# Last of seven products issued behind the next matrix's first product, with the weight factors placed anew

## The chip, the cores and the metric

The kernel runs on one core of one Trainium2 chip. The metric is the device time of one execution in microseconds (us), as the median of several runs; lower is better.

## The reference

The program is one inference step of a two-layer streaming encoder: feed-forward block, mixer, feed-forward block, and the same again with another mixer, on 640 tokens of width 1024. Four of the six sub-layers are feed-forward blocks, and the change lies in these alone. Each computes

```python
D_MODEL = 1024
D_FF = 2816
def swiglu(x, w_gate, w_up, w_down):
    return (jax.nn.silu(x @ w_gate) * (x @ w_up)) @ w_down
```

wrapped as x = LayerNorm(ALPHA * x + 0.5 * swiglu(x)). All arithmetic has float32 accuracy: a float32 factor is split into a high part and the remainder, and a product takes three matmuls (high by high, low by high, high by low).

## The kernel before, in words

The four blocks run one after the other as ffn0, ffn1, ffn2 and ffn3, with a mixer behind ffn0 and one behind ffn2. The hidden width 2816 is 22 rows f of 128 units. Rows 0 and 1 are done with plain products at the start of a block, and so is the gate of rows 2 and 3. Every other gate or up weight of two rows f and f + 1 is what the texts call a *matrix*: a 2 x 2 block problem (two rows of units, two halves of the 1024 inputs, two halves of the 640 tokens) that is done with seven products in place of eight. A block has 19 matrices, the four blocks have 76, and they are numbered here from 0: ffn0 has 0 to 18, ffn1 19 to 37, ffn2 38 to 56, ffn3 57 to 75. The first of each block is the up matrix of rows 2 and 3, and then gate and up alternate.

`operands` (L338) loads the two raw weight rows r0 and r1 (512 KB each, on SyncE's queue) and makes the seven weight factors: four halves as they come (b11, b21, b12, b22), and four differences that VectorE computes in place in the raw tiles (`total`, L348). A factor is then split (L99): ScalarE casts the high part (L100), VectorE subtracts it from the source (L101). `split2` does two factors at once, a cast and a subtraction of 1024 columns. The split factors lie in places that hold two factors each (`two_units`, pool "w", six places) and in one that holds a single factor (`unit`, pool "w1", one place).

`product` (L361) is 12 matmuls of 128 x 128 by 128 x 320 on TensorE (L365), into one PSUM bank. `matrix` (L369) runs the seven products in the order 1, 5, 6, 2, 7, 3, 4 over three banks: x takes products 1 and 2, w takes 5 and later 3, and z begins as a copy of x behind product 1 (`nc.scalar.copy`, L382, ScalarE) and then takes 6, 7 and 4. `keep` (L378) copies a bank to SBUF on ScalarE, behind product 5 and behind product 6. `take` hands a finished quarter to `gate` (add on VectorE, L407, then SiLU on ScalarE, L409) or `up` (L415 to L419, VectorE, and for a finished row its split, L261). The take behind product 7, L407 or L417, reads z, and product 4 then writes on into z. z alternates between two banks (`sums`); x and w come from pool "a", two banks.

`row_sums` (L444) follows an up matrix in ffn1 to ffn3, where the down projection too uses seven products: VectorE forms sums of the finished rows (L453 to L456), ScalarE and VectorE split them into `hs`. `tick` advances side work that ffn0 and ffn3 carry along. `down` (L535; `down7` in the later blocks) runs after every second pair of rows, between a gate and an up matrix. The first down of each block (rows 0 and 1, `tm_proj`, L216) stands directly ahead of the block's first matrix; its results are added to `yacc` on VectorE (L223).

The tile scheduler fixes each engine's order from the order of the code and its own estimate of the times; the engines then run their lists in order and wait for each other by semaphores.

Of the kernel before, what the change touches and what calls it, by code (L numbers as in the profile page):

```python
# [36 lines left out]
def kernel(ctx: ExitStack, tc: tile.TileContext, I, O, phases=PHASES):  # L37
# [45 lines left out]
    state = {"silu": None, "preload": None, "pst": bank_b}  # L83
# [15 lines left out]
    def split(hi, lo, src):  # L99
        nc.scalar.copy(hi, src)  # L100
        return nc.vector.tensor_tensor(lo, src, hi.bitcast(F32), op=ALU.subtract)  # L101

    def raw_tile():
        return pools["raw"].tile([128, 1024], F32, name="raw")
# [7 lines left out]
    def split2(w, src):  # L112

        return split(w[:, :, 0], w[:, :, 1], src.rearrange("p (j c) -> p j c", j=2))
# [111 lines left out]
    def ffn(i, ph, last, side=None):  # L226
# [4 lines left out]
        with ExitStack() as st:  # L231
# [3 lines left out]
            def tick(where):  # L235

                if ph == "ffn0" and where in range(NT):
                    for _ in range(2 if (fs[0], where) == (14, 4) else 1):
                        with tc.issue_after(state["acc"]):
                            next(steps, None)  # L240
                elif ph == "ffn3" and where in ("gate", "up", 0, 2, 4):
                    with tc.issue_after(state["silu"]):
                        next(steps, None)
# [34 lines left out]
            for h in range(2):  # L278
                o, L = HALVES[h]
# [14 lines left out]
            for r in range(2):  # L294
                with tc.issue_after(state["xc"]) if "xc" in state else ExitStack():
                    w = load_w(I["w_gate"][i, 2 + r])
# [41 lines left out]
            def operands(src0, src1):  # L338
                r0, r1 = raw_tile(), raw_tile()
                nc.sync.dma_start(r0, src0)  # L340
                nc.sync.dma_start(r1, src1)
                b11, b21, b12, b22 = r0[:, :512], r0[:, 512:], r1[:, :512], r1[:, 512:]
                u, v, w = (two_units() for _ in range(3))
                o = unit()

                def total(o, v, w):
                    with tc.issue_after(state["lo"]):
                        V.tensor_tensor(o, v, w, op=ALU.subtract)  # L348

                split2(u, r0)  # L350
                state["lo"] = split(v[:, 1, 0], v[:, 1, 1], b22).ins
                total(b11, b12, b11)
                split(v[:, 0, 0], v[:, 0, 1], b11)
                total(b12, b22, b12)
                total(b22, b22, b11)
                split2(w, r1)
                total(b21, b21, b22)
                split(o[:, 0], o[:, 1], b21)
                return {1: u[:, 0], 2: u[:, 1], 3: v[:, 1], 4: o, 5: v[:, 0], 6: w[:, 1], 7: w[:, 0]}

            def product(ps, A, p, first):  # L361
                n = 0
                for k in range(4):
                    for a, b in ((0, 0), (1, 0), (0, 1)):
                        nc.tensor.matmul(ps, A[p][:, a, k * 128:k * 128 + 128], X[p][b][:, k, :],  # L365
                                         start=(first and n == 0), stop=(n == 11), skip_group_check=True)
                        n += 1

            def matrix(A, take):  # L369

                z = sums[0]
                sums.reverse()
                x, w = (bank("a")[:, :Q] for _ in range(2))
                e = {}

                def keep(n, ps):
                    e[n] = wk.tile([128, Q], F32, name="mx", bufs=2)
                    nc.scalar.copy(e[n], ps)  # L378


                product(x, A, 1, True)
                nc.scalar.copy(z, x)  # L382
                product(w, A, 5, True)
                keep(5, w)
                product(z, A, 6, False)
                keep(2, z)
                product(x, A, 2, False)
                take(0, 0, x, None)
                product(z, A, 7, False)
                take(1, 1, z, e[5])  # L390
                product(w, A, 3, False)
                take(1, 0, w, e[2])
                product(z, A, 4, False)
                take(0, 1, z, None)

            def seven(f):
                return ph in SEVEN and f < NF - 4

            def pair(f, before=None):
                g = first if f == 2 else {}  # L400

                def gate(r, c, ps, e):
                    if r not in g:
                        g[r] = g_row()
                    t = g[r][:, Q * c:Q * c + Q]
                    if e is not None:
                        V.tensor_tensor(t, ps, e, op=ALU.add)  # L407
                        ps = t
                    state["silu"] = nc.scalar.activation(t, ps, AF.Silu).ins  # L409

                def up(r, c, ps, e):
                    c = slice(Q * c, Q * c + Q)
                    t = row(f + r)
                    if e is None:
                        V.tensor_tensor(t[:, c], ps, g[r][:, c], op=ALU.mult)  # L415
                    else:
                        V.tensor_tensor(t[:, c], ps, e, op=ALU.add)  # L417
                        if not c.start:
                            V.tensor_tensor(t, t, g[r], op=ALU.mult)  # L419
                    if r == 0 and c.start:  # L420
                        finish(f, *((256, T - 256) if seven(f) else (0, T)))
                    elif r == 1 and not c.start:
                        finish(f + 1)

                for n, take in (("w_gate", gate), ("w_up", up)):
                    if n == "w_gate" and f == 2:
                        tick("gate")
                        continue
                    if n == "w_up" and before is not None:
                        down(before)  # L430
                    with ExitStack() as q:
                        if f == 2:
                            for k in ("acc0", "xc"):
                                if k in state:
                                    q.enter_context(tc.issue_after(state[k]))
                        A = operands(I[n][i, f], I[n][i, f + 1])
                    if n == "w_up":
                        for r in range(2):
                            ht[f + r] = h_tile()
                    matrix(A, take)  # L440
                    if n == "w_up" and seven(f):
                        row_sums(f)
                    tick("gate" if n == "w_gate" else "up")

            hs = {}

# [110 lines left out]
            for c in range(5):  # L557
                done, fs = fs, list(range(2 + 4 * c, 6 + 4 * c))
                for f in fs[::2]:
                    pair(f, done if f == fs[0] else None)  # L560
            state["turn"] = 0
            down(fs, LN_OF[ph])

# [1448 lines left out]
```

## Time and profile before

| what | value |
|---|---|
| time, median of 3 runs | 2542.54 us (2541.85 to 2545.92) |
| time of the profiled execution | 2543.04 us |
| span in the profile | 2541.3 us |
| PE (TensorE matmul) busy | 2500.3 us, 98% of the span |
| DVE (VectorE) busy | 2015.3 us, 79% |
| ACT (ScalarE) busy | 1272.5 us, 50% |
| POOL (GpSimd) busy | 376.2 us, 15% |
| DMA | 324.80 MB, mean 128 GB/s |

A row of the timeline has the start in us from the span's start, the time that the merged instructions take, engine, line, operation, written tile <- read tiles with their shape, the number of instructions, and in brackets the idle time ahead and what ended it. PEld is TensorE's weight load, which runs beside the matmuls.

### The profile page before, as it was taken

The page shows a single profiled execution, that of the slowest core. Times are in us where ns is not written, and L with a number is a line of the kernel's source. Part 1 is how long each engine was busy: PE and PEld are TensorE (multiplying, and loading weights), DVE is VectorE, ACT ScalarE, POOL GpSimd, SP SyncE. Part 2 cuts the span into 40 slices and gives each one's busy share as a digit, 9 for nine tenths or more (in the row PEclk, how much of TensorE's full clock was granted, in tenths as well). Part 3 has the DMA queues.
Part 4 walks back from the last instruction along what each step waited for, and adds up shares of the span by engine and source line. Part 5 has one row for each costly group of instructions (what it writes and reads, how often), then busy time and mean ns, then how long its engine had stood idle before and what let it go on. Part 6 is the DMA issues. An engine that isn't in the chain of part 4 may idle for free. (4 is left out here: it accounts for less than half of the span.)

```text
span 2541.3 us, 40809 instructions
## 1 busy us (share of the span) xinstructions
PE 2500.3 (98%) x15551; PEld 2289.3 (90%) x15551; DVE 2015.3 (79%) x3505; ACT 1272.5 (50%) x2389; POOL 376.2 (15%) x492
## 2 busy tenths in 40 slices
PE   9999999999999999999999999999999999999998
PEld 9999999878789999999999999988989879999897
DVE  7788777666879888878988887777676689998887
ACT  4443444336744555553455554566565544554542
POOL 0000001210130000013000002211121152111121
PEclk9999999999999999999999999999999999999999
DMA  5332335443222433462144434466564722455563
GB/s 185 108 100 86 107 117 154 144 157 110 85 78 65 118 103 97 111 166 62 59 121 112 116 102 125 122 190 184 162 200 138 232 92 91 156 152 163 153 174 115
DMA packets 179253, 324.80 MB, mean 128 GB/s; under 512 B 21312, under 2 KB 92608, under 8 KB 178544
## 3 DMA queue, kind: packets, MB, share of 16 engines
q1 hardware_dynamic: 165200, 293.83, 36.8%
q0 software_dynamic: 13856, 28.35, 5.7%
q8 instruction: 122, 2.00, 0.3%
q14 instruction: 75, 0.61, 0.1%
HBM read 259.56 MB, written 40.54 MB: 118 GB/s over the span
## 5 line engine op out<-in xcount | busy, mean ns | idle before, releaser
L101 DVE TENSOR_TENSOR w<-raw,w 128x512 fp32r<-128x512 f32 (+2 forms) x721 | 625.0, 889 | 87.5 <-ACT w L100 84.7
L100 ACT CAST w<-raw 128x512 fp32r<-128x512 f32 (+1 forms) x721 | 531.8, 769 | 317.2 <-DVE raw L348 153.5
L365 PE MATMUL bank<-xhi,w 128*128 128x320 f32 x2432 | 540.4, 309 | 2.9 <-DVE s L407 1.9
L146 PE MATMUL bank<-xhi,w 128*128 128x256 f32 (+2 forms) x2272 | 499.9, 312 | 2.5 <-ACT xhi L100 1.5
L365 PE MATMUL bank<-T,w 128*128 128x320 f32 x2736 | 428.7, 309 | 3.0 <-ACT bank L382 1.6
L365 PEld LDWEIGHTS bank<-xhi,w 128*128 128x128 f32 x2432 | 406.6, 188 | 8.8 <-DVE s L407 3.1
L365 PEld LDWEIGHTS bank<-T,w 128*128 128x128 f32 x2736 | 407.0, 188 | 6.3 <-ACT bank L382 4.2
L146 PEld LDWEIGHTS bank<-xhi,w 128*128 128x128 f32 x2272 | 380.0, 189 | 11.9 <-issue 5.1
L365 PE MATMUL bank<-xlo,w 128*128 128x320 f32 x1216 | 375.0, 308 | 0.0
L146 PE MATMUL bank<-xlo,w 128*128 128x256 f32 (+2 forms) x1136 | 352.3, 311 | 1.9 <-DVE xlo L211 1.7
L146 PE MATMUL bank<-w,h 128*128 128x512 f32 x1488 | 346.5, 391 | 0.0
L146 PEld LDWEIGHTS bank<-w,h 128*128 128x128 f32 x1488 | 276.9, 188 | 57.6 <-ACT h L100 1.4
L365 PEld LDWEIGHTS bank<-xlo,w 128*128 128x128 f32 x1216 | 228.0, 187 | 0.0
L146 PEld LDWEIGHTS bank<-xlo,w 128*128 128x128 f32 x1136 | 215.0, 189 | 4.9 <-DVE xlo L211 2.0
L348 DVE TENSOR_TENSOR raw<-raw 128x512 f32<-128x512 f32 x304 | 212.4, 699 | 3.4
L514 POOL DMA_DIRECT2D yacc<-ev x84 | 72.7, 889 | 688.2 <-ACT ev L513 603.0
L501 PE MATMUL bank<-w,h 128*128 128x512 f32 x576 | 134.5, 389 | 0.0
L501 PEld LDWEIGHTS bank<-w,h 128*128 128x128 f32 x576 | 108.1, 188 | 22.5
L378 ACT COPY mx<-bank 128x320 f32<-128x320 f32 x152 | 64.6, 425 | 103.7 <-PE bank L365 103.4
L510 DVE SCALAR_TENSOR_TENSOR yacc<-bank,yacc 128x512 f32<-128x512 f32 x84 | 57.8, 688 | 72.2 <-PE bank L501 72.1
L223 DVE SCALAR_TENSOR_TENSOR yacc<-bank,yacc 128x512 f32<-128x512 f32 x120 | 81.8, 686 | 34.3 <-PE bank L146 33.8
L513 ACT ACTIVATE ev<-bank 128x512 f32<-128x512 f32 x84 | 50.1, 597 | 115.8 <-PE bank L501 113.3
(431 smaller groups left out, 3436.7 us busy)
## 6 DMA issues: line engine op xcount, KB each, us to landing
raw<-in_w_gate_dram SPq DMA_DIRECT2D x88, 512.0 KB, 3.7
raw<-in_w_up_dram SPq DMA_DIRECT2D x88, 512.0 KB, 3.9
raw<-in_w_down_dram SPq DMA_DIRECT2D x88, 512.0 KB, 3.6
raw<-in_m_in_dram SPq DMA_DIRECT2D x52, 512.0 KB, 4.6
yacc<-ev POOLq DMA_DIRECT2D x84, 256.0 KB, 4.5
raw<-in_m_out_dram SPq DMA_DIRECT2D x24, 512.0 KB, 4.3
csb<-cs_d SPq DMA_DIRECT2D x20, 512.0 KB, 5.1
h<-in_ssd_h_dram SPq DMA_DIRECT2D x16, 512.0 KB, 6.1
```

Source lines behind the costliest of these rows:

```text
L100: nc.scalar.copy(hi, src)
L101: return nc.vector.tensor_tensor(lo, src, hi.bitcast(F32), op=ALU.subtract)
L146: state["pe"] = nc.tensor.matmul(ps, a, b, start=(k == 0), stop=(k == n - 1)).ins
L223: state["acc"] = nc.vector.scalar_tensor_tensor(ya, pb, scale, ya, op0=ALU.mult, op1=ALU.add).ins
L348: V.tensor_tensor(o, v, w, op=ALU.subtract)
L365: nc.tensor.matmul(ps, A[p][:, a, k * 128:k * 128 + 128], X[p][b][:, k, :], start=(first and n == 0), stop=(n == 11), skip_group_check=True)
L378: nc.scalar.copy(e[n], ps)
L501: nc.tensor.matmul(ps, a[:, u], b[:, v], start=(first and n == 0), stop=(n == 5), skip_group_check=True)
L510: V.scalar_tensor_tensor(ya, ps, 0.5 / ALPHA, ya, op0=ALU.mult, op1=ALU.add)
L513: nc.scalar.mul(e, ps, 0.5 / ALPHA)
L514: nc.gpsimd.dma_start(yacc[:, t, 512 * j:512 * j + 512], e, accum_op=ALU.add)
```

## The change

Product 4 of a matrix, its take and what follows it (row sums, tick) are put into a function, `last_product`, and held in the list `rest`. The next matrix calls it (`complete`) behind its own product 1 and the copy to z, so that TensorE runs 1 of the next matrix, then 4 of this one, then 5 of the next. Ahead of a `down`, and behind the last matrix, `complete` runs at once, so there product 4 stays where it was.

The factors change places. Product 1's factor (b11) moves into the single place; products 2 and 3 share one double place, products 5 and 4 another (one cast and one subtraction of 1024 columns, from r0 after all its differences), products 7 and 6 the third. The four differences now come all in a row, ahead of the two double splits. The counts of splits, differences, matmuls and loads are the same.

```diff
-                split2(u, r0)
-                state["lo"] = split(v[:, 1, 0], v[:, 1, 1], b22).ins
+                split(o[:, 0], o[:, 1], b11)
+                split(u[:, 0, 0], u[:, 0, 1], b21)
+                state["lo"] = split(u[:, 1, 0], u[:, 1, 1], b22).ins
                 total(b11, b12, b11)
-                split(v[:, 0, 0], v[:, 0, 1], b11)
                 total(b12, b22, b12)
                 total(b22, b22, b11)
+                total(b21, b21, b22)
+                split2(v, r0)
                 split2(w, r1)
-                total(b21, b21, b22)
-                split(o[:, 0], o[:, 1], b21)
-                return {1: u[:, 0], 2: u[:, 1], 3: v[:, 1], 4: o, 5: v[:, 0], 6: w[:, 1], 7: w[:, 0]}
+                return {1: o, 2: u[:, 0], 3: u[:, 1], 4: v[:, 1], 5: v[:, 0], 6: w[:, 1], 7: w[:, 0]}
...
-            def matrix(A, take):
+            rest = []
+
+            def complete():
+                if rest:
+                    rest.pop()()
+
+            def matrix(A, take, after):
...
                 product(x, A, 1, True)
                 nc.scalar.copy(z, x)
+                complete()
                 product(w, A, 5, True)
...
-                product(z, A, 4, False)
-                take(0, 1, z, None)
+
+                def last_product():
+                    product(z, A, 4, False)
+                    take(0, 1, z, None)
+                    after()
+
+                rest.append(last_product)
...
                     if n == "w_up" and before is not None:
+                        complete()
                         down(before)
...
-                    matrix(A, take)
-                    if n == "w_up" and seven(f):
-                        row_sums(f)
-                    tick("gate" if n == "w_gate" else "up")
+
+                    def after(up=n == "w_up"):
+                        if up and seven(f):
+                            row_sums(f)
+                        tick("up" if up else "gate")
+
+                    matrix(A, take, after)
...
+            complete()
             state["turn"] = 0
             down(fs, LN_OF[ph])
```

How the instructions stand on the engines, at three places. The first is TensorE in ffn0, at the end of matrix 0 and the start of matrix 1. bank_394 is matrix 0's z, bank_845 (before) or bank_830 (after) matrix 1's x, T1, T2 and T4 are the token factors of products 5, 6 and 3. Before:

```order
240 L365 MATMUL bank_722<-T4_516,w_702 128x320 x12
241 L365 MATMUL bank_394<-xhi_82,w1_704 128x320 x2
242 L365 MATMUL bank_394<-xlo_83,w1_704 128x320
...
249 L365 MATMUL bank_845<-xhi_82,w_827 128x320 x2
250 L365 MATMUL bank_845<-xlo_83,w_827 128x320
...
257 L365 MATMUL bank_846<-T1_514,w_828 128x320 x12
258 L365 MATMUL bank_395<-T2_515,w_829 128x320 x12
```

And after the change:

```order
240 L365 MATMUL bank_722<-T4_516,w_701 128x320 x12
241 L365 MATMUL bank_830<-xhi_82,w1_815 128x320 x2
242 L365 MATMUL bank_830<-xlo_83,w1_815 128x320
...
249 L365 MATMUL bank_394<-xhi_82,w_702 128x320 x2
250 L365 MATMUL bank_394<-xlo_83,w_702 128x320
...
257 L365 MATMUL bank_831<-T1_514,w_813 128x320 x12
258 L365 MATMUL bank_395<-T2_515,w_814 128x320 x12
```

Matrix 0's product 4 into bank_394 moved from ahead of matrix 1's product 1 to behind it: a whole product stands between product 3 and product 4, and two products stand between matrix 1's product 1 and its product 6, which writes the copied z (bank_395).

The second place is VectorE at the start of ffn0's first matrix. raw_697 and raw_698 are r0 and r1; w_701, w_702 and w_703 are the places u, v and w, w1_704 is the single place; yacc is the first down's result. Before:

```order
79 L101 TENSOR_TENSOR w_701<-raw_697,w_701 128x2x512
80 L223 SCALAR_TENSOR_TENSOR yacc_84<-bank_649,yacc_84 128x512
81 L101 TENSOR_TENSOR w_702<-raw_698,w_702 128x512
...
83 L348 TENSOR_TENSOR raw_697<-raw_698,raw_697 128x512
...
87 L101 TENSOR_TENSOR w_702<-raw_697,w_702 128x512
88 L223 SCALAR_TENSOR_TENSOR yacc_84<-bank_681,yacc_84 128x512
89 L348 TENSOR_TENSOR raw_698<-raw_698,raw_697 128x512
90 L223 SCALAR_TENSOR_TENSOR yacc_84<-bank_689,yacc_84 128x512
91 L348 TENSOR_TENSOR raw_697<-raw_697,raw_698 128x512
92 L101 TENSOR_TENSOR w_703<-raw_698,w_703 128x2x512
```

And after the change:

```order
79 L101 TENSOR_TENSOR w1_704<-raw_697,w1_704 128x512
80 L223 SCALAR_TENSOR_TENSOR yacc_84<-bank_649,yacc_84 128x512
81 L101 TENSOR_TENSOR w_701<-raw_697,w_701 128x512
82 L101 TENSOR_TENSOR w_701<-raw_698,w_701 128x512
83 L223 SCALAR_TENSOR_TENSOR yacc_84<-bank_657,yacc_84 128x512
84 L348 TENSOR_TENSOR raw_697<-raw_698,raw_697 128x512
...
90 L348 TENSOR_TENSOR raw_697<-raw_697,raw_698 128x512
91 L223 SCALAR_TENSOR_TENSOR yacc_84<-bank_689,yacc_84 128x512
92 L101 TENSOR_TENSOR w_702<-raw_697,w_702 128x2x512
93 L101 TENSOR_TENSOR w_703<-raw_698,w_703 128x2x512
```

The split that product 5 reads (w_702 from raw_697) moved from row 87, behind one difference, to row 92, behind all four and behind the last accumulation into yacc.

The third place is ScalarE in ffn1, where the row sums of an up matrix (h, ev, hs) meet the gate matrix that follows it; bank_7729 is that gate's z, mx_8925 and mx_8939 are the kept products 5 and 6. Before:

```order
622 L100 CAST h_8760<-hf_8830 128x640
623 L100 CAST h_8759<-hf_8816 128x384
624 L382 COPY bank_7729<-bank_8898 128x320
625 L100 CAST h_8759<-ev_8864 128x256
626 L100 CAST hs_8869<-ev_8863 128x512
627 L378 COPY mx_8925<-bank_8899 128x320
628 L100 CAST hs_8869<-ev_8864 128x256
629 L378 COPY mx_8939<-bank_7729 128x320
```

And after the change (the lines have moved: L388 is the copy to z, L384 the kept copy):

```order
629 L388 COPY bank_7729<-bank_8870 128x320
630 L100 CAST w1_8991<-raw_8984 128x512
631 L100 CAST h_8760<-hf_8830 128x640
632 L100 CAST h_8759<-hf_8816 128x384
633 L384 COPY mx_8925<-bank_8871 128x320
634 L100 CAST hs_8906<-ev_8900 128x512
635 L100 CAST h_8759<-ev_8901 128x256
636 L100 CAST hs_8906<-ev_8901 128x256
637 L384 COPY mx_8939<-bank_7729 128x320
```

The casts of the finished row moved from ahead of the copy to z to behind it. The kept copy of product 6 stays behind the last of them.

## The prediction

> **What bounds the kernel now.** I read the page's first lines, then the line of the products by itself with what it waited for, then the timeline of TensorE around the longest waits. The page and the groups:
>
> ```profile
> span 2541.3 us, 40809 instructions
> PE 2500.3 (98%) x15551; PEld 2289.3 (90%) x15551; DVE 2015.3 (79%) x3505; ACT 1272.5 (50%) x2389; POOL 376.2 (15%) x492
> L365 PE MATMUL bank<-xhi,w 128*128 128x320 f32 x2432 | 540.4, 309 | 2.9 <-DVE s L407 1.9
> L365 PE MATMUL bank<-T,w 128*128 128x320 f32 x2736 | 428.7, 309 | 3.0 <-ACT bank L382 1.6
> ```
>
> TensorE is busy 98% of the span, and the change leaves the number and the sizes of its matmuls alone. So all that it can win is time in which TensorE waits inside the matrices, and all that it can lose is new waits there. What the line of the products waited for, weight loads included (us, times):
>
> ```profile
>   ACT bank L382: 5.8, 13
>   DVE s L407: 5.0, 9
>   ACT mx L378: 2.5, 6
>   DVE hf L417: 2.1, 9
>   DVE w L101: 2.0, 3
>   ACT w L100: 1.4, 2
> ```
>
> Three kinds: the copy to z (L382), which product 6 needs; the takes behind product 7 (L407, L417), which product 4 needs; the factors (L100, L101). The change touches all three. TensorE in matrix 62 shows the first two:
>
> ```profile
> 2249.29 1.92 PE L365 MATMUL bank<-T,w 128*128 128x320 f32 x12
> 2251.36 2.03 PE L365 MATMUL bank<-T,w 128*128 128x320 f32 x12 [0.15 <-ACT bank L382]
> 2253.22 0.46 PE L365 MATMUL bank<-xhi,w 128*128 128x320 f32 x2
> ...
> 2256.74 1.92 PE L365 MATMUL bank<-T,w 128*128 128x320 f32 x12
> 2259.12 0.56 PE L365 MATMUL bank<-xhi,w 128*128 128x320 f32 x2 [0.46 <-DVE s L407]
> 2259.52 0.31 PE L365 MATMUL bank<-xlo,w 128*128 128x320 f32 x1
> ```
>
> A product without a wait takes 1.92 us from its first start to its last end, with an overlap: 11 distances and one matmul of 0.309, so 0.1465 per distance and 1.76 us from one product's start to the next. Product 5 starts at 2249.29, product 6 at 2251.36: 2.07, so 0.31 late, and it runs 0.10 longer (2253.22 - 2251.36 = 1.86), since the second matmul too starts late behind a wait. The copy costs 0.41. Product 3 starts at 2256.74, product 4 at 2259.12: 2.38, so 0.62 late, and its first two matmuls take 0.40 in place of 0.29, 0.11 more. The take costs 0.73, where the idle column shows 0.46. I add up distances between starts: by the idle column alone the two waits of this matrix would be worth 0.61 instead of 1.14, and the sum below about half. The Trainium skill, "Perfetto Trace Analysis", section "Per-instruction lifecycle: what the profiler-reported window actually captures", states that the profiler estimates a matmul's end from its size and does not observe it. The trace agrees: the idle 0.46 stands beside 0.73 of distance.
>
> **The change part by part.** *Product 4 one product later.* I read all 76 matrices in this way. Fifteen have a late product 4, and they lose 5.2 us together; four of them 0.73 to 0.77 each, two 0.42 and 0.49, the other nine at most 0.16. The last of the four:
>
> ```profile
> 2413.30 0.56 PE L365 MATMUL bank<-xhi,w 128*128 128x320 f32 x2 [0.47 <-DVE s L407]
> ```
>
> All fifteen are in matrices with no down behind them, so each gets a whole product, 1.76 us, of cover, and the largest lateness is 0.67. I count all of it: -5.2. If the next product 1 were itself late, TensorE would wait there, but its factor is now the first that is split. *Product 6 behind its copy.* Matrix 0 and six gates in ffn3 (2251.36 is the first, 2432.50 the last) lose 3.5 us to the copy to z. In the six gates product 4 of the matrix ahead now fills 1.76 us between copy and need, and the largest lateness there is 0.60; matrix 0 loses only 0.23, and its product 5 comes later anyway (below). So -3.5. Together -8.7.
>
> *Factor of product 5 later.* This is the price. Its split now waits for all four differences. Inside a block the factors are made some 2.5 us or more ahead of their use, but a block's first matrix starts as soon as the first down's matmuls are done, while VectorE still adds their results (L223). ffn0, VectorE, then TensorE:
>
> ```profile
> 59.56 1.22 DVE L101 TENSOR_TENSOR w<-raw,w 128x1024 fp32r<-128x1024 f32 x1
> 60.69 0.69 DVE L223 SCALAR_TENSOR_TENSOR yacc<-bank,yacc 128x512 f32<-128x512 f32 x1
> 61.29 0.68 DVE L101 TENSOR_TENSOR w<-raw,w 128x512 fp32r<-128x512 f32 x1
> ...
> 67.29 0.68 DVE L348 TENSOR_TENSOR raw<-raw 128x512 f32<-128x512 f32 x1
> 67.95 3.56 DVE L101 TENSOR_TENSOR w<-raw,w 128x1024 fp32r<-128x1024 f32 x4
> ```
>
> ```profile
> 67.88 3.90 PE L365 MATMUL bank<-T,w 128*128 128x320 f32 x24
> 71.62 0.45 PE L365 MATMUL bank<-xhi,w 128*128 128x320 f32 x2
> ```
>
> VectorE runs without a gap: 0.60 per instruction of 512 columns, 1.13 per one of 1024. The new order has from 59.56 on thirteen of 512 ahead of product 5's split, the fourth difference as the twelfth: it starts at 59.56 + 11 x 0.60 = 66.16 and ends 0.68 later, at 66.84. Then ScalarE's cast of 1024 columns:
>
> ```profile
> 1258.74 1.06 ACT L100 CAST w<-raw 128x1024 fp32r<-128x1024 f32 x1
> ```
>
> 1.06, and VectorE's split, 1.22: done at 69.1 or, with the handovers, 69.2. Product 5 is due at 67.88, and its second matmul takes the low part: 69.2 - 68.0 = 1.2, with the restart 1.3 lost. ffn1:
>
> ```profile
> 808.92 0.69 DVE L223 SCALAR_TENSOR_TENSOR yacc<-bank,yacc 128x512 f32<-128x512 f32 x1
> 809.53 0.68 DVE L348 TENSOR_TENSOR raw<-raw 128x512 f32<-128x512 f32 x1
> 810.28 0.69 DVE L223 SCALAR_TENSOR_TENSOR yacc<-bank,yacc 128x512 f32<-128x512 f32 x1
> ```
>
> ```profile
> 811.85 3.38 PE L365 MATMUL bank<-T,w 128*128 128x320 f32 x22
> ```
>
> Here VectorE waits for the down's matmuls, and the fourth difference takes the slot at 809.53: end 810.2, cast 811.3, split 812.5, against 812.0 when the second matmul is due: 0.5 late, 0.65 with the restart, and the same in ffn2, whose order is the same. ffn3 already pays for its factors at the start, in matrices 57 and 58:
>
> ```profile
> 2157.54 0.46 PE L365 MATMUL bank<-xhi,w 128*128 128x320 f32 x2
> ...
> 2161.05 0.45 PE L365 MATMUL bank<-xhi,w 128*128 128x320 f32 x2
> 2162.21 0.41 PE L365 MATMUL bank<-T,w 128*128 128x320 f32 x1 [0.56 <-ACT w L100]
> ...
> 2175.45 0.46 PE L365 MATMUL bank<-xhi,w 128*128 128x320 f32 x2
> 2176.78 1.88 PE L365 MATMUL bank<-T,w 128*128 128x320 f32 x11 [0.73 <-DVE w L101]
> ```
>
> Product 1 of matrix 57 starts at 2157.54. The rows at 2161.05 and 2175.45, each with the matmul behind it, take 0.44: 1.16 - 0.44 = 0.72 and 1.33 - 0.44 = 0.89 late, with restarts 1.07 and 1.24, 2.3 together. Afterwards the scheduler puts product 2 ahead of product 5 in matrix 57, and I place its split's end by the same slots at 2162.7 against 2161.2: 1.5 lost, 1.65 with the restart, and matrix 58's factors, now split in one piece, up to half a microsecond late or not at all. So -0.5.
>
> Sum: -8.7 + 1.3 + 0.65 + 0.65 - 0.5 = -6.6 us. Bounds: if the starts cost nothing, and ffn3's fall away, -8.7 - 2.3 = -11.0; if at all four starts another split of 1024 slips in between, as 1.13 each, -2.1. I stay near the middle, as the order's rows fix the places.
>
> The rest is work that moves without gain. The row sums come one product later, with their ScalarE casts behind the copy to z; the loads keep their count, and only SyncE's wait for a free raw tile moves with the splits. Engines beside TensorE have room:
>
> ```profile
> 1241.00:1304.00 63.00, 63.00 (x373) 58.79 (x372) 52.98 (x82) 34.47 (x57) 5.22 (x6) 1.00 0.41 108
> 2160.00:2235.00 75.00, 73.71 (x435) 68.06 (x434) 67.71 (x101) 39.36 (x65) 15.54 (x13) 1.00 0.54 162
> ```
>
> (length, then PE, PEld, DVE, ACT and POOL busy): VectorE 84% in ffn1 and 2, 90% at ffn3's start.
>
> **The rivals.** *The starts take back most.* TensorE keeps its order, so all that stands behind a late product 5 is late with it. At 2162.21 one matmul of another product waited and product 2's next matmuls, on a factor used since 2157.54, stood behind it. The Trainium skill, "TensorE: Matmul & The Clock Gate", Part 3, section "The mechanism", has the rule: matmuls start and end in program order; the trace agrees, by that 0.72. With the extra split at four starts: 2543.04 - 2.1 = 2540.9, as a median 2540.4. For it: VectorE runs gapless at 59.56 to 71; against: the order of the rows.
>
> *The waits only move, since VectorE bounds ffn3.* About 2.8 of the 5.2 and 3.3 of the 3.5 lie in ffn3. If VectorE at 90% were the bound there, TensorE would wait for the same instructions one product on; -8.7 + 6.1 + 2.6 = 0: 2542.5. Against: it needs VectorE full for the whole block, and the late takes are late by 0.6, not by more each matrix.
>
> *Slower: the row sums hold up the kept copy of product 6.* Row sums are formed 24 times:
>
> ```profile
> L453 DVE TENSOR_TENSOR ev<-hf x24: 409/416/426, 823.8 to 2427.8; 128x256 f32<-128x256 f32 x24
> ```
>
> In the 24 gates behind them ScalarE's kept copy, which product 7 waits for, stands behind the casts of the sums. The chain in ffn1 and ffn2 goes from the take to the last cast:
>
> ```profile
> 1267.65 0.48 DVE L415 TENSOR_TENSOR hf<-bank,s 128x320 f32<-128x320 f32 x1
> ```
>
> ```profile
> 1271.22 0.41 ACT L100 CAST hs<-ev 128x256 fp32r<-128x256 f32 x1
> ```
>
> 1271.63 - 1267.65 = 3.98 us. Now it starts when product 4 ends, with products 5, 6 and 2 behind: 3 x 1.76 = 5.28, less the copy's 0.42: 4.86. So 0.88 to spare. If one weight cast of 1024 and one of 512 columns (1.06 and 0.62) fall into the chain, it is 5.66, and each of the 24 loses 0.8: +19.2 - 6.6 = +12.6, a median of 2555.1. It decides from 0.88 on, and makes the kernel slower by 0.2% from (5.1 + 6.6) / 24 = 0.5 more per gate. For it: ffn3's chain needs more room beside its side work. Against: the rows of the new order have no weight cast inside it.
>
> **How the numbers follow.** A measurement of this kernel can tell about 0.2%, 5.1 us, from no change. The profiled execution lies 0.5 above the median, so the forecast is 2543.04 - 6.6 - 0.5 = 2535.9; I say 2536.0. Chances: forecast 0.58 (2532 to 2538), starts take back most 0.21, waits only move 0.13, slower 0.08. The forecast's low end, -11.0, gives 2531.5; the range leaves out its last half microsecond and the slower case, and takes in the two middle ones: 2532.0 to 2542.8. Faster by over 0.2% means below 2537.5: nearly the whole forecast case, 0.55. Within: the rest of it, the starts and the moved waits, 0.37. Slower: 0.08.
>
> **What would show it.** Right: product 4 without a wait in the next matrix, no idle time for the copy to z in ffn3's gates behind another matrix, and a wait of 1.3, 0.65 and 0.65 for L101 in product 5 of matrices 0, 19 and 38. The forecast is wrong if these starts lose over 2 us each, if product 7 waits for the kept copy (now L384) in ffn1 and ffn2, or if waits of the size of the old ones stand at product 5 or 6 instead.

## The result and the profile after

The changed kernel takes 2547.26 us (median of 12 runs, 2542.48 to 2549.81), the kernel before 2540.57 us in the same runs (median of 12, 2537.82 to 2545.92). The ratio is 1.0021, 95% interval 1.0013 to 1.0028: slower by 0.13 to 0.28%, about 5.3 us by the ratio (the two medians lie 6.7 apart), where 6.6 us less was forecast and a time of 2532.0 to 2542.8. The profiled execution took 2544.83 us.

The page of the changed kernel, its first lines and the groups of the products:

```profile
span 2543.1 us, 40801 instructions
PE 2495.1 (98%) x15551; PEld 2283.3 (90%) x15551; DVE 2031.1 (80%) x3505; ACT 1270.3 (50%) x2389; POOL 372.4 (15%) x492
L365 PE MATMUL bank<-xhi,w 128*128 128x320 f32 x2432 | 539.6, 309 | 5.5 <-ACT mx L384 2.6
L365 PE MATMUL bank<-T,w 128*128 128x320 f32 x2736 | 427.1, 309 | 3.3 <-DVE w L101 1.8
L517 PE MATMUL bank<-w,h 128*128 128x512 f32 x576 | 136.3, 391 | 3.1 <-DVE yacc L526 2.6
```

The old releasers, the takes and the copy to z, no longer lead these rows; three others do: the kept copy (L384), the factors (L101), and the addition to yacc in the seven-product down (L526), a line that had no wait in the profile before. What the products waited for (us, times; L388 is now the copy to z, L419 the gate's take, L429 the up's):

```profile
  ACT mx L384: 7.4, 12
  DVE s L419: 4.9, 8
  DVE w L101: 4.6, 7
  ACT w L100: 3.4, 4
  ACT bank L388: 1.4, 2
  DVE hf L429: 1.1, 3
```

And the down's line:

```profile
  DVE yacc L526: 6.7, 7
  ACT ev L529: 2.1, 4
```

The spans of two profiles differ also where the change does nothing, so I compare the four blocks, each from the first to the last start of a product (us), with the waits of TensorE in them, added up by distances between starts as in the prediction:

| | ffn0 | ffn1 | ffn2 | ffn3 | waits, all | waits in ffn3 |
|---|---|---|---|---|---|---|
| before | 358.1 | 331.8 | 331.8 | 347.1 | 15.0 | 9.4 |
| after | 357.7 | 332.4 | 332.4 | 352.6 | 21.1 | 14.8 |

The blocks are 6.4 us longer, and the waits in them 6.1. (The expectation of e5 below has 16.6 and 22.7 for all waits; the difference is the same.) The stretches between the blocks are 4.5 us shorter in this profile (2.1 of it ahead of the first matrix), which is why its span is only 1.8 longer. ffn3 alone carries 5.5 of the 6.4.

Inside ffn3 the 14.8 us are: the kept copy 4.4 us (0.9 before), the gates' takes ahead of a down 3.0 (0 before), the two places where the deferred product 4 still waits for an up's take 0.85, the down 4.7 (0 before), and the start 1.8 (2.3 before). Of the start, 0.25 in matrix 57 stands in every profile of this case, also in that of e8 below, where almost nothing else is lost at the start; the forecast counted it as a restart. TensorE in matrix 64, a gate behind an up matrix with row sums; product 7 starts at 2279.66, product 3 at 2281.52, product 4 (a down follows) at 2283.76:

```profile
2278.41 0.45 PE L365 MATMUL bank<-xhi,w 128*128 128x320 f32 x2
2279.66 0.56 PE L365 MATMUL bank<-xhi,w 128*128 128x320 f32 x2 [0.64 <-ACT mx L384]
...
2281.52 1.92 PE L365 MATMUL bank<-T,w 128*128 128x320 f32 x12
2283.76 0.56 PE L365 MATMUL bank<-xhi,w 128*128 128x320 f32 x2 [0.32 <-DVE s L419]
```

2279.66 - 2278.41 = 1.25 where 0.44 is due: 0.80 late, and product 4 0.48. GpSimd and VectorE ahead of that:

```profile
2272.44 2.06 POOL L1503 TENSOR_TENSOR h<-h,el 128x512 f32<-128x512 f32 x1 [26.48 <-DMA h<-in_ssd_h_dram]
2275.60 1.22 POOL L1503 TENSOR_TENSOR h<-h,el 128x512 f32<-128x512 f32 x1 [1.10 <-DVE hf L427]
```

```profile
2273.52 1.67 DVE L101 TENSOR_TENSOR h<-hf,h 128x640 fp32r<-128x640 f32 x1
2275.10 0.48 DVE L427 TENSOR_TENSOR hf<-bank,s 128x320 f32<-128x320 f32 x1
2275.51 0.41 DVE L469 TENSOR_TENSOR ev<-hf 128x256 f32<-128x256 f32 x1
2275.84 1.26 DVE L471 TENSOR_TENSOR ev<-hf 128x256 f32<-128x256 f32 x1
```

And VectorE at the like place of ffn2 (matrix 41), where there is no side work:

```profile
1265.80 0.82 DVE L101 TENSOR_TENSOR h<-hf,h 128x640 fp32r<-128x640 f32 x1
1266.54 0.48 DVE L427 TENSOR_TENSOR hf<-bank,s 128x320 f32<-128x320 f32 x1
1266.94 0.42 DVE L469 TENSOR_TENSOR ev<-hf 128x256 f32<-128x256 f32 x1
1267.27 0.42 DVE L471 TENSOR_TENSOR ev<-hf 128x256 f32<-128x256 f32 x1
```

The same split takes 1.67 beside the multiplication and 0.82 alone, the same subtraction 1.26 and 0.42: 1.7 us in one chain, more than the 0.88 that the prediction found to spare. In ffn1 and ffn2 the kept copy came in time and product 7 did not wait.

### The profile page after: what moved, and what is told of

It reads as the page before. It is cut to its first block, busy times and chain, and to the rows that moved or that the text cites. A ratio compares the mean times of both kernels' runs of the same rounds, so it can differ in the third digit from the quotient of the medians.

```text
span 2543.1 us, 40801 instructions
## 1 busy us (share of the span) xinstructions
PE 2495.1 (98%) x15551; PEld 2283.3 (90%) x15551; DVE 2031.1 (80%) x3505; ACT 1270.3 (50%) x2389; POOL 372.4 (15%) x492
## 5 line engine op out<-in xcount | busy, mean ns | idle before, releaser
L101 DVE TENSOR_TENSOR w<-raw,w 128x512 fp32r<-128x512 f32 (+1 forms) x721 | 629.8, 896 | 131.5 <-ACT w L100 126.4
L146 PE MATMUL bank<-w,h 128*128 128x512 f32 x1488 | 346.5, 391 | 0.0
L384 ACT COPY mx<-bank 128x320 f32<-128x320 f32 x152 | 64.2, 424 | 88.5 <-PE bank L365 88.3
L146 PE MATMUL bank<-w,og 128*128 128x512 f32 x432 | 105.2, 399 | 2.5 <-DVE og L101 1.8
L223 DVE SCALAR_TENSOR_TENSOR yacc<-bank,yacc 128x512 f32<-128x512 f32 x120 | 81.7, 685 | 26.1 <-PE bank L146 25.0
```

The costliest lines, as they stand in the source:

```text
L146: state["pe"] = nc.tensor.matmul(ps, a, b, start=(k == 0), stop=(k == n - 1)).ins
L223: state["acc"] = nc.vector.scalar_tensor_tensor(ya, pb, scale, ya, op0=ALU.mult, op1=ALU.add).ins
```

## The experiments

The table has all experiments. Each time stands beside that of the kernel before, measured with it; the last column is the waits in ffn3, counted as in the table above:

| run | us (before) | ratio, 95% | ffn0 | ffn1 | ffn2 | ffn3 | waits ffn3 |
|---|---|---|---|---|---|---|---|
| e1_p5_early | 2540.31 (2541.44) | 0.9999 [0.999, 1.0007] | 355.4 | 331.6 | 331.7 | 350.6 | 12.7 |
| e2_factors_only | 2557.86 (2541.44) | 1.0068 [1.0054, 1.0082] | 362.7 | 332.8 | 332.9 | 362.2 | 24.4 |
| e3_sums_later | 2542.4 (2541.44) | 1.0006 [0.9998, 1.0015] | 357.3 | 332.3 | 332.3 | 348.0 | 10.2 |
| e4_gates_only | 2562.01 (2541.44) | 1.0083 [1.0069, 1.0097] | 358.2 | 332.5 | 332.5 | 363.1 | 25.2 |
| e5_defer_only | 2610.05 (2541.61) | 1.0276 [1.0262, 1.029] | 367.5 | 346.0 | 346.5 | 366.6 | 28.2 |
| e6_defer_sums_later | 2609.99 (2541.61) | 1.0274 [1.026, 1.0288] | 367.9 | 344.1 | 343.4 | 365.7 | 27.4 |
| e7_side_on_vector | 2536.14 (2541.61) | 0.9981 [0.9972, 0.999] | 359.1 | 332.6 | 332.3 | 341.9 | 4.1 |
| e8_before_side_on_vector | 2531.48 (2541.61) | 0.9965 [0.9952, 0.9977] | 358.5 | 331.8 | 331.8 | 338.2 | 0.5 |
| e9_early_side_vector | 2530.41 (2540.55) | 0.996 [0.9947, 0.9973] | 355.3 | 331.6 | 331.6 | 338.7 | 0.7 |
| e10_idle_products | 2556.99 (2540.55) | 1.0065 [1.0053, 1.0077] | 358.0 | 331.8 | 331.8 | 363.1 | 25.3 |
| e11_factors_side_vector | 2541.78 (2540.55) | 1.0006 [0.9998, 1.0015] | 362.4 | 332.8 | 332.8 | 343.7 | 5.8 |
| e12_memsets | 2540.2 (2541.71) | 0.9995 [0.9986, 1.0004] | 358.2 | 331.8 | 331.8 | 347.0 | 9.3 |
| e13_two_products | 2544.71 (2541.71) | 1.0016 [1.0007, 1.0025] | 359.3 | 331.8 | 331.8 | 350.7 | 12.8 |

**e1_p5_early.** Product 5's factor by itself, early:

```diff
                 total(b11, b12, b11)
+                split(v[:, 0, 0], v[:, 0, 1], b11)
...
-                split2(v, r0)
                 split2(w, r1)
+                total(b21, b21, b22)
+                split(v[:, 1, 0], v[:, 1, 1], b21)
```

> The changed kernel, but product 5's factor is split by itself right behind the first difference, and product 4's by itself behind the last (one cast and one subtraction more per matrix). The changed kernel ran 5.3 us over the kernel before by the ratio 1.0021. Theory A (the price is the late factor of product 5 at the starts of the blocks): the waits for L100 and L101 at matrices 0, 19 and 38 (2.5, 0.73, 0.73 us in the changed kernel) go, 3.9 us less, so +1 to +2 us against before. Theory B (the price is in ffn3, where the row sums hold up the kept copy and product 4 ahead of a down waits for its take): the starts gain the same 3.9, but the waits for L384 (4.4 us) and L419 (3.0 us) in ffn3 stay as they are. If only A were true these would go as well.

Measured: no difference from before that can be told, so some 5 us under the changed kernel. ffn0, ffn1 and ffn2 are 2.6, 0.1 and 0.1 us shorter than before: with the starts mended, the deferral wins there what it was meant to win. The waits for the kept copy in ffn3 stayed (4.8), and ffn3 is still 3.5 us longer than before. So the late factor was a part of the price, 3.8 us in ffn0 to ffn2 against the changed kernel, and ffn3 holds the rest.

**e2_factors_only.** The operands of the changed kernel, the products of the kernel before.

> The kernel before with the new places and the new order of the factors alone: product 4 stays directly behind product 3. Theory B (deferring the product brings the row sums onto the kept copy): no wait for the kept copy of product 6 in ffn3 beyond before's 0.9 us, the old waits for the copy to z (3.5 us) and for the takes (5.2 us) stay, and the starts cost 2.5 + 0.7 + 0.7 as in the changed kernel: +3 to +4 us against before. Theory C (four differences in one run and the double splits block VectorE, and so everything in ffn3 is late): the waits in ffn3 for the kept copy and the waits in the seven-product down for the addition to yacc (4.7 us) appear here too: +8 us or more.

Measured: 17 us slower, ffn3 15 us longer; no wait for the kept copy in ffn3 (it was 0.9), but 14.5 us in the down. The down's line waited for

```profile
  DVE yacc L510: 17.4, 6
  ACT ev L513: 4.8, 7
```

with nothing listed there before. By the size this is theory C, but its reason is not the right one, as e11 shows.

**e3_sums_later.** The row sums behind the next matrix's kept copy of product 6:

```diff
                 keep(2, z)
+                if later:
+                    later.pop()()
                 product(x, A, 2, False)
...
-                    after()
+                    later.append(after)
```

> The changed kernel, but what follows product 4's take (row sums and tick) is issued behind the kept copy of product 6 of the next matrix, so that ScalarE's list has that copy ahead of the casts of the row sums. Theory B: the waits for L384 in ffn3 (4.4 us) go, and with them part of the 3.0 us at product 4 ahead of a down: 4 to 7 us less than the changed kernel, so +1 to -2 us against before. Theory A: no difference from the changed kernel, +5 us, since the starts are the same.

Measured: +1.5 us by the ratio, not told from before. The waits for the kept copy in ffn3 fell from 4.4 to 0.9, the starts stayed. So the row sums do hold up that copy, and theory B explains the part it was about; the takes ahead of a down (2.8) and the down (4.3) stayed.

**e4_gates_only.**

```diff
                     matrix(A, take, after)
+                    if n == "w_up":
+                        complete()
```

> The changed kernel, but only a gate's product 4 is put behind the next matrix's product 1; an up matrix is completed at once. Theory B: the row sums run as before, so the waits for the kept copy go (4.4 us) and those at product 4 ahead of a down shrink; the copy to z in the gates of ffn3 waits again (3.3 us), since no product 4 is ahead of it; the takes of the gates stay covered. Net some 3 us less than the changed kernel: about +2 us against before. Theory A: the starts are the same, and the copy to z comes back: +8 us.

Measured: 21 us slower, missed by both theories. The waits for the kept copy fell (to 1.6), but the down in ffn3 now cost some 16 us. So the deferral of an up matrix moves more than its row sums. What it moves ahead of the down's additions on VectorE no run takes apart.

**e5_defer_only** and **e6_defer_sums_later.** The deferral with the factors in the order of before, product 3's factor in the single place:

```diff
                 split2(u, r0)
-                state["lo"] = split(v[:, 1, 0], v[:, 1, 1], b22).ins
+                state["lo"] = split(o[:, 0], o[:, 1], b22).ins
...
-                split(o[:, 0], o[:, 1], b21)
+                split(v[:, 1, 0], v[:, 1, 1], b21)
```

> Product 4 deferred as in the change, but the factors in the order of the kernel before: first one split of 1024 columns for products 1 and 2, product 5's factor behind the first difference, product 4's as the last. Only two places are exchanged: product 3's factor takes the single place, product 4's the half beside product 5's. Waits of TensorE inside the feed-forward stretches, added up by start distances, were 16.6 us in the kernel before (of which ffn3 9.4) and 22.7 in the changed one (ffn3 14.8). Theory D (the new order of the factors is the costly half, the deferral the useful one): the starts' 3.9 us are not there, the waits at the down's additions to yacc in ffn3 (4.7) are not there, the takes and the copy to z are covered, and only the kept copy (up to 5) and the takes ahead of a down (2 to 3) in ffn3 remain: about 10 us of waits, -4 to -7 us against before. Theory B (the deferral itself is bad in ffn3): -1 to +3 us against before, ffn3 as long as in the changed kernel.

> The same as e5_defer_only, and what follows product 4's take (row sums, tick) issued behind the kept copy of product 6 of the next matrix. Theory D and B both say that the kept copy's waits go (4.4 us less to 1.0 in the changed kernel when this alone was done): some 3 to 4 us under e5_defer_only, so -7 to -10 us against before by D, -2 to -4 by B.

Measured: both some 69 us slower, in all blocks, far outside what either theory allows. Something else decides here, so the two runs do not tell D from B. ScalarE, then TensorE, in ffn1 of e5_defer_only:

```profile
910.01 0.62 ACT L100 CAST w<-raw 128x512 fp32r<-128x512 f32 x1 [4.85 <-PE bank L365]
911.46 0.73 ACT L100 CAST h<-hf 128x640 fp32r<-128x640 f32 x1 [0.83 <-DVE hf L431]
```

```profile
908.05 1.92 PE L365 MATMUL bank<-T,w 128*128 128x320 f32 x12
```

The cast into the single place waits 4.85 us, until product 3 (on T4), which reads that place, is done at 909.97; all behind it on ScalarE waits too. ScalarE's waits of this kind in ffn1 (us in total, times, longest), e5 and then the changed kernel:

```profile
ACT w L100 <- PE bank L365: 51.8, 14, 4.8
```

```profile
ACT w L100 <- PE bank L365: 15.4, 18, 3.1
```

More than three times as much. With the deferral and product 3's factor in the single place, the next matrix's cast waits for product 3. The change avoids this by giving the place to product 1, so this part of it is no extra; other ways to avoid it were not run.

**e7_side_on_vector** and its control **e8_before_side_on_vector**, one edit in each kernel:

```diff
-                nc.gpsimd.tensor_tensor(h4, h4, el8[:, g, 4 * h + 2 * b2 + q, :, None].to_broadcast([128, 8, 64]),
+                nc.vector.tensor_tensor(h4, h4, el8[:, g, 4 * h + 2 * b2 + q, :, None].to_broadcast([128, 8, 64]),
```

> The changed kernel with the 32 multiplications of ffn3's side work (128 x 512, 1.0 to 2.3 us each on GpSimd) done by VectorE instead. Theory E (the two engines hinder each other: VectorE's split of 640 columns took 1.67 us beside such a multiplication and 0.82 without): the row sums' chain in ffn3 gets shorter by up to 1.7 us each, the waits for the kept copy (4.6 us) and at the additions to yacc (3.5 us) shrink by half or more, -3 to -6 us against the changed kernel. Theory F (VectorE is simply full in ffn3): 32 x 0.6 = 19 us more work for it there, and ffn3 gets longer by some us.

> The kernel before with the same 32 multiplications on VectorE, as the control for e7_side_on_vector. Theory E: here too ffn3 waits less (of its 9.4 us of waits the 3.4 for the copy to z and the 2.2 for the takes shrink): -2 to -4 us. Theory F: longer by some us.

Measured: 10 us less for the changed kernel (1.0021 to 0.9981), 9 us less for the kernel before. That is theory E, with twice the gain that it expected or more; theory F falls. The four kernels in ffn3, in the order before, after, e8, e7 (length, then PE, PEld, DVE, ACT and POOL busy):

```profile
2157.50:2505.00 347.50, 342.49 (x2056) 319.73 (x2056) 302.63 (x446) 178.08 (x296) 63.41 (x59) 1.00 0.55 158
```

```profile
2153.80:2506.80 353.00, 344.07 (x2057) 319.65 (x2056) 308.69 (x444) 178.55 (x296) 62.53 (x58) 1.00 0.53 156
```

```profile
2154.80:2493.30 338.50, 338.50 (x2056) 319.74 (x2055) 305.91 (x474) 177.35 (x296) 25.68 (x30) 1.00 0.55 162
```

```profile
2155.70:2498.00 342.30, 340.90 (x2056) 319.91 (x2055) 305.85 (x473) 177.78 (x296) 25.59 (x30) 1.00 0.55 160
```

VectorE does 28 instructions more in e8 than before and is busy only 3.3 us longer, mostly since no other of its instructions is stretched any more: in ffn3 of the kernel before 18 were lengthened by 11.2 us in sum, after the change 23 by 17.0, here none. (The sum alone does not set the price: in e1 it is 21.5 us, and ffn3 is 2.0 us shorter than in the changed kernel.) In e7 the kept copy and the takes ahead of a down cost nothing, and the down 0.6 us where it had cost 4.7. And the waits of ffn3 in the kernel before, 9.4 us, are down to 0.5: what the change set out to cover in ffn3 was made by the side work on GpSimd, and with it gone there is nothing to cover. Then the changed kernel is 4.7 us slower than the other (2536.14 against 2531.48), mostly by its starts. So the side work makes both the waits that the change removes in ffn3 and the new ones that it brings there; the loss by the starts stays without it.

**e9_early_side_vector**: e1's and e7's edits together.

> The deferral with product 5's factor split early (as in e1_p5_early) and the side work's multiplications on VectorE (as in e7_side_on_vector). Theory E (GpSimd's multiplications make ffn3's waits): ffn0 to ffn2 as in e1_p5_early (355.4, 331.6, 331.7 us, 2.6 + 0.1 + 0.1 under before), ffn3 as in e8_before_side_on_vector, 338.2, so some 2 to 3 us under e8_before_side_on_vector and 12 to 13 under before. If the deferral is bad in ffn3 by itself, ffn3 stays near the 341.9 of e7_side_on_vector, and the time near e8's, -10.

Measured: 0.4% under before, the fastest of all, but not told apart from e8 (0.996 and 0.9965, intervals overlap). Against e8 its blocks win 3.1 us in ffn0 and 0.2 each in ffn1 and ffn2 and lose 0.5 in ffn3. The deferral is not bad in ffn3 by itself. What the products still waited for in it:

```profile
  ACT bank L389: 1.3, 2
  ACT mx L385: 0.2, 1
```

**e11_factors_side_vector**: e2's and e8's edits together.

> The factors' new places and order alone (as in e2_factors_only, +17 us) with the side work's multiplications on VectorE. Theory E: the 16 us of waits in ffn3's seven-product downs and takes go, and only the starts (2.5 + 0.7 + 0.7 + about 1.5) and the waits of ffn0's takes remain: +5 to +7 us against e8_before_side_on_vector, -3 to -5 against before. If the run of single splits is bad in itself, ffn3 stays over 350 us and the time over before's.

Measured: 10 us over e8, more than expected, ffn3 343.7 where e2 had 362.2. Of the 14.5 us that e2 lost in ffn3's down 1.9 are left, so most of those came with the side work on GpSimd too. Over e8 it is 3.9 us in ffn0, 0.9 and 1.0 in ffn1 and ffn2 and 5.5 in ffn3, where the start and the copy to z wait.

**e10_idle_products, e12_memsets, e13_two_products**: e8's kernel with work on GpSimd put back that nobody waits for. (e12 fills the place in which the identity stood.)

```diff
+                with tc.issue_after(m.ins):
+                    nc.vector.memset(one, 1.0)
+                for _ in range(4):
+                    nc.gpsimd.tensor_tensor(ident, ident, one.to_broadcast([128, 128]), op=ALU.mult)
                 pst = state["pst"]()
```

> The kernel of e8_before_side_on_vector with work on GpSimd put back that nobody waits for: behind each of the 32 multiplications on VectorE, GpSimd multiplies the 128 x 128 identity by ones four times. GpSimd is as busy as before, but no result of the side work comes from it. Theory E1 (it is the two engines' working side by side that slows VectorE): VectorE's instructions get longer beside these, ffn3 gets back a good part of the 9 us of waits that it had before, +3 to +9 us against e8_before_side_on_vector. Theory E2 (it is the side work's chain through GpSimd, or the accumulating DMAs queued behind its multiplications): the first is gone, so at most the queued DMAs remain, and the time stays near e8's (-10 us against before).

> The kernel of e8_before_side_on_vector, and behind each of the 32 multiplications on VectorE nine fills of the 128 x 128 identity's place on GpSimd, which read nothing (the identity is not used any more by then). GpSimd's list is about as full as in the kernel before, with the same accumulating DMAs queued behind. Theory E1 (GpSimd's reading beside VectorE's two-operand reading lengthens VectorE): VectorE's instructions keep their lengths, ffn3 stays at 338 to 341 us, the time within 3 us of e8's, about -8 to -10 us against before. Theory E2 (the DMAs queued behind GpSimd's work hold up ScalarE's evictions): ffn3 gets longer by 5 us and more, waits for the evictions on ScalarE in the seven-product down.

> As e10_idle_products, but two products of the identity in place of four behind each multiplication, so that GpSimd's side work (about 50 us) is near the 44.5 us of the kernel before. E1: VectorE's instructions get longer as in the kernel before (11 us in ffn3), ffn3 goes to 345 to 350 us, the time to about that of before (-4 to +2 us). E2: the same as e12_memsets, since the lists are equally full.

GpSimd's groups in e10, e12 and e13:

```profile
L1492 POOL TENSOR_TENSOR ident<-ident,one 128x128 f32<-128x128 f32 x128 | 101.6, 794 | 245.9 <-DVE one L1490 238.9
```

```profile
L1494 POOL MEMSET ident<- 128x128 f32 x288 | 63.9, 222 | 14.2
...
L1491 POOL TENSOR_TENSOR one<-one 128x1 f32<-128x1 f32 x32 | 21.4, 670 | 232.5 <-DVE one L1490 232.5
```

```profile
L1492 POOL TENSOR_TENSOR ident<-ident,one 128x128 f32<-128x128 f32 x64 | 49.8, 779 | 266.8 <-DVE one L1490 264.3
```

All three lose what e8 had won, or more. VectorE's instructions in ffn3 are lengthened by 10.6 us in e10 (53 of them), 5.8 in e13 (27), 0 in e12. In e12, whose fills read nothing, ffn3 is still 347.0: of its waits 4.0 us are evictions of the down on ScalarE (L514), 1.7 additions to yacc, and 2.7 takes of up matrices.

So lengthening is not the only way from GpSimd's work to TensorE. Another is GpSimd's list: the down's accumulating DMAs are issued from it, and while such a DMA is under way its source is a place that ScalarE evicts into. Over ffn3 the profile lists 25.0 us of evictions waiting for these DMAs in e12, against 7.6 in e8 (1.4 in the kernel before, 19.6 in the changed one). One wait stands only in the two runs with lengthened instructions: in matrices 64, 68 and 72 product 4 waits about 0.75 us each for a gate's take in e10 and 0.34 in e13, and not at all in e8 and e12.

The sizes cannot be taken from these three runs. In each, VectorE's write of `one` waits once for GpSimd, for 5.4 us in e10, 4.3 in e12 and 5.0 in e13, inside the first seven-product down of ffn3, an effect of the added code. Without that down e12 has 2.0 us of waits for evictions. Nor is GpSimd's load the same: its added work is 101.6 us in e10, 85 in e12 and 49.8 in e13, where the multiplications of the kernel before take 44.5. And the work was put back into e8's kernel only, not into e7's. How the changed kernel's waits divide between the two ways stays open.

## Why the prediction was wrong

*The waits that were counted as gone (-8.7).* They went, but for 0.85 us: no gate of ffn3 behind another matrix waits for the copy to z, and of fifteen late products 4 two remain late. This mechanism was right. e1 shows the gain where nothing else is in the way: ffn0 2.6 us shorter.

*The starts (+2.6 with ffn0 to ffn2, -0.5 in ffn3).* ffn1 and ffn2 were right (0.73 each, 0.65 forecast), and so was ffn3 (2.3 to 1.8). ffn0 was mis-sized: 2.5 us for 1.3. TensorE and VectorE there:

```profile
64.04 0.45 PE L365 MATMUL bank<-xhi,w 128*128 128x320 f32 x2
...
67.10 0.41 PE L365 MATMUL bank<-T,w 128*128 128x320 f32 x1 [1.14 <-ACT w L100]
68.36 3.63 PE L365 MATMUL bank<-T,w 128*128 128x320 f32 x23 [0.85 <-DVE w L101]
```

```profile
58.69 0.68 DVE L101 TENSOR_TENSOR w<-raw,w 128x512 fp32r<-128x512 f32 x1
...
67.08 3.56 DVE L101 TENSOR_TENSOR w<-raw,w 128x1024 fp32r<-128x1024 f32 x4 [0.51 <-ACT w L100]
```

By the prediction's count the fourth difference and the cast end at 67.90 in the old profile's time; this profile began the row 0.87 earlier (58.69 for 59.56), which gives 67.03, and the split began at 67.08. But TensorE began the matrix 2.1 earlier (64.04 for 66.12), and VectorE only 0.87. The size of such a wait is the difference of two engines' places, and one profile gives only one sample of it. The one used was an extreme: in the 15 profiles of this case the matrix starts between 62.9 and 66.1, and 66.12 is the latest. In e8, the same kernel up to ffn3, it starts at 63.52, and the copy to z costs 1.14 us in matrix 0 instead of 0.23.

*The step that failed.* "The rest is work that moves without gain ... Engines beside TensorE have room": new waits inside ffn3 got no term in the sum. The third rival looked at them. It priced the moved row sums by the chain of ffn1 and ffn2 (3.98 us, 0.88 to spare), noted that the chain of ffn3 "needs more room beside its side work", and did not work that room out. The rows were in the profile: in ffn3 before, 18 of VectorE's instructions were lengthened beside the side work. Its reason against, "the rows of the new order have no weight cast inside it", did not hold either. ScalarE in matrix 41 of ffn2 and in matrix 64 of ffn3 has a weight cast of 1024 columns there, just ahead of the chain's first cast in the one (at 1267.37) and behind it in the other (at 2275.62):

```profile
1266.41 1.05 ACT L100 CAST w<-raw 128x1024 fp32r<-128x1024 f32 x1 [0.64 <-PE bank L365]
2276.04 1.05 ACT L100 CAST w<-raw 128x1024 fp32r<-128x1024 f32 x1
```

In ffn1 and ffn2 there was room even so, and the kept copy never made product 7 wait; in ffn3 one or two lengthened instructions of 0.85 each use the room up. Counted in ffn3: kept copy +3.4, takes ahead of a down +3.0, down +4.7, together 11.1 us that had no term. All but 0.6 of it is gone in e7, where the side work's multiplications are not on GpSimd (four small waits of 0.28, in matrices 61, 65, 69 and 73, are new there). With this term the sum is -8.7 + 0.85 + 2.5 + 1.5 - 0.5 + 11.1 = +6.75. Small waits elsewhere, most of them in ffn0, are some 0.65 less, which leaves the 6.1 by which the waits grew; the blocks are 6.4 longer. The prediction's signs of being wrong named the kept copy in ffn1 and ffn2 and the starts, so the stage that lost the time was not among the places to look at.

*The down's part* (4.7) had no rival at all. In the new order two splits of 512 columns stand on VectorE's list ahead of one of the down's last additions, and their casts stand behind ScalarE's evictions; before, that addition stood ahead of the first split and waited only for TensorE:

```profile
2226.64 0.69 DVE L510 SCALAR_TENSOR_TENSOR yacc<-bank,yacc 128x512 f32<-128x512 f32 x1 [2.03 <-PE bank L501]
```

The changed kernel there, VectorE, then TensorE:

```profile
2224.83 1.81 DVE L101 TENSOR_TENSOR w<-raw,w 128x512 fp32r<-128x512 f32 x1 [2.12 <-ACT w L100]
2226.57 0.68 DVE L526 SCALAR_TENSOR_TENSOR yacc<-bank,yacc 128x512 f32<-128x512 f32 x1
...
2230.88 1.41 DVE L348 TENSOR_TENSOR raw<-raw 128x512 f32<-128x512 f32 x2
2232.21 0.68 DVE L526 SCALAR_TENSOR_TENSOR yacc<-bank,yacc 128x512 f32<-128x512 f32 x1
```

```profile
2232.95 1.65 PE L517 MATMUL bank<-w,h 128*128 128x512 f32 x6 [1.21 <-DVE yacc L526]
```

The split waits 2.12 for its cast and then takes 1.81 where 0.68 is usual; the additions behind it come late, and TensorE waits 1.21 for the one at 2232.21 before it may write that bank again. Without GpSimd's side work the same order costs 0.6 us in the down (e7). Not all of it is the stretching: the cast stood behind an eviction that had waited 2.52 us for an accumulating DMA, which took 8.1 us to land where 4.8 is the median. No multiplication ran on GpSimd in that time, and why this DMA was slow stays open.

*The rivals.* "The waits only move, since VectorE bounds ffn3" had the place right and the reason wrong: VectorE was given 28 instructions more there (e8) and ffn3 got 9 us shorter. "Slower: the row sums hold up the kept copy" was the right mechanism in one block of three, and 3.4 us of the loss, not 19. "The starts take back most" needed 6.6 us at the four starts; they cost 3.5, where the forecast had 2.1.

## What to carry to other kernels

Before a wait is covered by moving work, look whether its cause can be removed instead: ask first why the waited-for engine is late in this stage and not in its twin (here ffn3 against ffn1), by comparing the durations of the same instructions in both. Moved work is to be priced with the durations of the stage in which it lands, the worst one. And an engine with a low busy share (GpSimd, 15%) can make the waits of a full one (TensorE, 98%).

## What the runs showed of the hardware

Beside one of the side work's multiplications on GpSimd (by more than 0.05 us of overlap) the changed kernel has 61 instructions of VectorE. Of the 47 that read two operands from SBUF 24 are lengthened by over 0.1 us, the most by 1.13; of the 14 that read a PSUM bank as one operand (L427 and L526 among them) none. All 24 began inside a multiplication, and each is longer by what was left of that multiplication, less 0.13 to 0.15 us; of the other 23 most had begun ahead of it. The Trainium skill, "SBUF — State Buffer", section "SBUF: two separate sides", states this rule: a VectorE instruction with two SBUF inputs and a GpSimd instruction that reads SBUF exclude each other on a shared pair of ports for a whole instruction. The trace agrees, as does e12, in which GpSimd's fills read nothing and lengthened none.
